# Weighted one-hot matrices built on VectorE alone, and expert products, row gathers and their pace moved between the last three stages

## The chip, the cores and the metric

The kernel runs on one core of a Trainium2 chip. A core has TensorE (PE; its weight loads are listed apart as PEld), VectorE (DVE), ScalarE (ACT), GpSimd (POOL) and SyncE (SP), and 16 DMA engines. Plain transfers are issued from SP's queue, indirect gathers from POOL's. The metric is device microseconds of one execution; the figure for a version is the median of its runs.

## The reference

A two-layer transformer block is followed by a second block, whose last part is the mixture of experts below. Everything that the change touches lies there. 512 tokens (s) have width 1024 (d); there are 8 heads, 128 x 128 = 16384 experts, and 16 experts are picked for each token and head.

```
def peer_ffn(h, w_query, sub_keys, expert_u, expert_v):
    ...
        q = (x_blk @ w_query).reshape(b, t, PEER_HEADS, 2, HALF_KEY)
        scores = jnp.einsum('bthcd,hcnd->bthcn', q, sub_keys).astype(jnp.float32)
        top_s, top_i = lax.top_k(scores, PEER_TOPK)
        cand_s = top_s[..., 0, :, None] + top_s[..., 1, None, :]
        cand_i = top_i[..., 0, :, None] * N_KEYS + top_i[..., 1, None, :]
        ...
        best_s, pos = lax.top_k(cand_s, PEER_TOPK)
        expert_idx = jnp.take_along_axis(cand_i, pos, axis=-1)
        gate = jax.nn.softmax(best_s, axis=-1)
        u = expert_u[expert_idx]
        v = expert_v[expert_idx]
        act = jax.nn.gelu(jnp.einsum('btd,bthkd->bthk', x_blk, u).astype(jnp.float32), approximate=False)
        return jnp.einsum('bthk,bthkd->btd', (gate * act).astype(v.dtype), v)
```

## The kernel before

Everything is float32; a product is made of three matmuls on a high and a low part (`split`: ScalarE rounds the high part, VectorE or GpSimd subtracts it to get the low part). The four blocks of 128 tokens are treated in two ways.

- The first block (object `PA`, `NG = 1`) **gathers**: for each of its 8 x 16 picks an indirect DMA on POOL's queue (`gather`, L1517) brings 128 rows of `peer_u` (one for each token, 128 x 1024 f32, 0.52 MB) into a tile `u`, and VectorE multiplies and sums them with the token rows (`score`, L1531). After 128 of these come `weights`, and 128 gathers of `peer_v` rows that VectorE adds up (`combine`, L1596). The tiles come from a ring of `UD = 4` buffers. The gathers keep their order on POOL (`in_order`).
- The other three blocks (`NV = 3`, 384 tokens) are **dense**. `scores` multiplies all 16384 rows of `peer_u` with the tokens, in 32 groups of 512 experts: a group is two calls of `load_w` with two halves of 128x1024 each (tiles `raw`, `whi`, `wlo`; in this stage GpSimd makes the `wlo` of one half and VectorE that of the other) and 2 x 2 x 8 x 3 = 96 matmuls of 384 columns. The scores go to DRAM (`Sd`). `one_hots` turns the picks into a weight matrix: for four tokens at a time (96 batches) VectorE compares an index row `iota` with the two key indices (`oe`, `oq`, 128 x 4 x 128), ScalarE scales `oe` by the weight, token by token, and TensorE multiplies the two (L1564, 8 matmul records a batch). The result goes to DRAM (`Gd`). `experts` then loads, for each group, the weights (`gt`) and scores (`s`), multiplies them (L1655), splits them (`gh`, `gl`), splits four 128x1024 slices of `peer_v` (`vh`, `vl`) and runs 4 x 3 x 2 x 3 = 72 matmuls of 512 columns (L1682 to L1684) into six PSUM banks that are kept to the end.

The code is written by generators that take turns: `alongside(main, others)` always advances the one with the smallest ratio of steps done to its number, and ends with `main`. Three such stages end the program:

```
        alongside((PB.queries(), 91), (scores_, S_1), (gather_a, G_1))
        alongside((spread(), 69 * NV), (scores_, S_2), (gather_a, G_2))
        for _ in scores_:
            pass
...
        alongside((experts(fp), 32 * 9), (gather_a, max(10, G_3 - G_1 - G_2)))
```

They are called here the **queries** stage (routing of the last two blocks: products with `w_query`, top-16 searches and decoding on VectorE, tiles `ts`, `cand`, `oh`), the **spread** stage (one-hots) and the **experts** stage. `scores` has two steps a group, so `S_1, S_2 = 20, 40` puts 10 groups beside the queries and 20 beside the one-hots; `G_1, G_2, G_3 = 60, 80, 260` do the same for the gathers. A scheduler then sets the final order on each engine; it moves instructions by its own estimate of when they are ready.

Of the kernel before, what the change touches and what calls it, by code (L numbers as in the profile page):

```python
# [14 lines left out]
AF = mybir.ActivationFunctionType  # L15
OP = mybir.AluOpType
AX = mybir.AxisListType
PSUM = bass.MemoryType.PSUM

NO_SYNC = mybir.DependencyInfo(mybir.DependencyClass.NoSync, mybir.DependencyReason.DATA)  # L20

S, D, KT = 512, 1024, 8
# [29 lines left out]
UB = 6  # L52
F_1, F_2, F_3, F_4, L_4 = 1, 36, 2, 20, 1
L_A = 0.01
S_1, S_2, G_1, G_2, G_3 = 20, 40, 60, 80, 260
N_1 = 0
ORD = 1
NU = 32
NG = 1
NV = S // 128 - NG  # L60
# [131 lines left out]
def build(tc, A, out, stop=None, dump=None):  # L192
# [3 lines left out]
    with ctx:  # L196
# [37 lines left out]
        def in_order(i):  # L234
            tc.keep_in_program_order(i)
# [319 lines left out]
        with tc.tile_pool(name="l0", bufs=1) as lp:  # L555
# [97 lines left out]
            for g in range(4):  # L653

                src, n = us[g], 1
# [729 lines left out]
        def normed(q0, w, xh, xl, xs_=None):  # L1385
# [17 lines left out]
            for k in range(KT):  # L1403
# [2 lines left out]
                split(xh[:, k], xl[:, k], h)  # L1406
                yield

        class Peer:
            def __init__(self, h, xh, xl, pool, ng):  # L1410
                self.xh, self.xl, self.ng = xh, xl, ng
                self.q0, self.t0, self.sl = h.q0, h.t0, h.sl
                self.h2 = [hp.tile([128, D], F, name="h2", bufs=ng) for _ in range(ng)]
                self.sd = [pe.tile([128, 8, 16], F, name="sd", bufs=ng) for _ in range(ng)]
                self.ix = [pe.tile([128, 8, 16], I32, name="ix", bufs=ng) for _ in range(ng)]
                self.bs, self.i1, self.i2 = ([pool.tile([128, 8, 16], F, name=n, bufs=2) for _ in range(NT)]
                                             for n in ("bs", "i1", "i2"))
                self.idx, self.ti, self.bp = {}, {}, {}

            def rows(self, t):  # L1420
# [93 lines left out]

            def gather(self, table, t, hd, j):
                u = ring[0]()
                i = GP.indirect_dma_start(out=u, out_offset=None, in_=A[table],  # L1517
                                          in_offset=bass.IndirectOffsetOnAxis(ap=self.idx[t, hd][:, j:j + 1], axis=0))
                if ORD:
                    in_order(i)  # L1520
                return u

            def score(self):
# [26 lines left out]
            def one_hots(self, t):  # L1550
# [17 lines left out]
                for c in range(4):  # L1568
                    st = dp.tile([128, 128, 32], F, name="st", bufs=2)
                    for b in range(8):  # L1570
                        q = dp.tile(full, F, name="oq", bufs=3)
                        e = dp.tile(full, F, name="oe", bufs=3)
                        cut = slice(c * 32 + b * 4, c * 32 + b * 4 + 4)
                        io = iota[:, None, :].to_broadcast(full)
                        V.tensor_tensor(e, io, T[:, 0, cut][:, :, None].to_broadcast(full), op=OP.is_equal)
                        for n in range(4):
                            SC.activation(e[:, n], e[:, n], AF.Copy, scale=T[:, 2, cut][:, n:n + 1])
                        V.tensor_tensor(q, io, T[:, 1, cut][:, :, None].to_broadcast(full), op=OP.is_equal)
                        pend.append((q, e, st[:, :, b * 4:b * 4 + 4]))
                        yield  # L1580
                        if len(pend) > 1:
                            finish()
                        yield
# [44 lines left out]
        def experts(pl):  # L1628
# [43 lines left out]
            def products(g):  # L1672

                gh, gl, vs = st.pop(g)
                for e in range(4):
                    h, l = vs[e]
                    end = g == order[-1] and e == 3
                    for t in range(NV):
                        ts = slice(t * 128, t * 128 + 128)
                        for c in range(2):  # L1680
                            p, cs = acc[t][c], slice(c * 512, c * 512 + 512)
                            PE.matmul(p, gh[:, e, ts], h[:, cs], start=False, stop=False, skip_group_check=True)  # L1682
                            PE.matmul(p, gh[:, e, ts], l[:, cs], start=False, stop=False, skip_group_check=True)  # L1683
                            PE.matmul(p, gl[:, e, ts], h[:, cs], start=False, stop=end, skip_group_check=True)  # L1684
                            if end:
# [83 lines left out]
        dps.close()  # L1769
        fin_ = ExitStack()  # L1770
        fp = fin_.enter_context(tc.tile_pool(name="fp", bufs=1))
        alongside((experts(fp), 32 * 9), (gather_a, max(10, G_3 - G_1 - G_2)))
        for _ in gather_a:
            pass
        fin_.close()
# [28 lines left out]
```

## Time and profile before

| | us |
|---|---|
| median of 3 runs (range) | 3069.81 (3062.46 to 3075.19) |
| the profiled execution | 3066.25 |
| its span, first to last instruction | 3064.5 |
| PE busy in the span | 2896.3 (95%) |
| DVE, ACT, POOL busy in the span | 2155.9 (70%), 1374.7 (45%), 1153.7 (38%) |
| queries stage, first product with `yh` to the end of decoding | 1785 to 2105 |
| spread stage, to the last score product | 2105 to 2508 |
| experts stage, first product to the last | 2514 to 3061 |
| POOL's wait in the experts stage for VectorE to give back a ring buffer | 172.5 |

Matmuls are pipelined and a busy PE need not be PE at its peak: the distance between the starts of equal matmuls tells more than their share of busy time. A duration printed by the trace overlaps the next instruction's by some 0.08 us on DVE, so there too the distance between starts is what an instruction occupies.

### The profile page before, as it was taken

The numbers are of one execution on the slowest core, as the hardware profiler recorded it, in microseconds if no ns is written. First come the engines' busy times: TensorE is split into PE (matmuls) and PEld (weight loads), VectorE is DVE, ScalarE is ACT, GpSimd is POOL, SyncE is SP. The second block draws the span as 40 slices with busy tenths as digits, with TensorE's granted clock in tenths as the row PEclk, the third lists the DMA queues.
The fourth block names the chain that finished last, engine by engine and source line by source line (L and its number), as shares of the span: only waits on it lengthen the run. The fifth ranks groups of instructions, "written<-read, shape, count | busy, mean of one in ns | idle before, by whom it ended". The sixth has DMA issues, their size and how long they took to land.

```text
span 3064.5 us, 44596 instructions
## 1 busy us (share of the span) xinstructions
PE 2896.3 (95%) x16770; PEld 2545.5 (83%) x16770; DVE 2155.9 (70%) x3873; ACT 1374.7 (45%) x2363; POOL 1153.7 (38%) x722
## 2 busy tenths in 40 slices
PE   8999999999989898989789989889999999999999
PEld 6568888878789898789787689889999998777887
DVE  6854344498766737658985668998778758888753
ACT  4533223477454545444354433346666643333332
POOL 3110000344310475467554146555555444454200
PEclk9999999999999999999999889999999999999999
DMA  3122232311245443235342058777787889999964
GB/s 132 41 77 96 87 106 85 101 69 42 62 166 191 162 145 111 83 135 181 120 147 87 18 183 301 248 260 281 294 296 278 302 321 385 371 375 377 333 226 145
DMA packets 195881, 568.29 MB, mean 185 GB/s; under 512 B 16944, under 2 KB 68528, under 8 KB 194000
## 3 DMA queue, kind: packets, MB, share of 16 engines
q1 hardware_dynamic: 157664, 427.61, 40.1%
q0 software_dynamic: 37712, 137.71, 12.1%
q8 instruction: 132, 2.16, 0.3%
q14 instruction: 85, 0.70, 0.1%
q10 hardware_dynamic: 288, 0.11, 0.0%
HBM read 512.93 MB, written 52.43 MB: 184 GB/s over the span
## 4 chain that ended last, share of the span: by engine, by line
PE 72%; DVE 16%; issue 3%; DMA 3%; ACT 3%; POOL 1%; SPq 0%; ACTq 0%; POOLq 0%; DVEq 0%
PE ps L269 15%; PE ps L271 15%; PE ps L270 15%; PE ps L1683 5%; PE ps L1684 5%; PE ps L1682 5%; PE ps L1564 3%; DVE wlo L232 2%; DVE u L1531 2%; POOL wlo L232 1%; PE ps L487 1%; DMA u<-in_peer_u_dram,ix 1%; DMA u<-in_peer_v_dram,ix 1%; PE ps L1173 1%; DVE nm L457 1%
## 5 line engine op out<-in xcount | busy, mean ns | idle before, releaser
L232 POOL TENSOR_TENSOR wlo<-raw,whi 128x1024 fp32r<-128x1024 f32 (+2 forms) x240 | 589.7, 2465 | 597.6 <-ACT whi L231 550.9
L231 ACT ACTIVATE whi<-raw 128x1024 fp32r<-128x1024 f32 (+2 forms) x518 | 515.6, 998 | 634.9 <-PE ps L270 366.2
L232 DVE TENSOR_TENSOR wlo<-raw,whi 128x1024 fp32r<-128x1024 f32 (+3 forms) x278 | 346.9, 1249 | 220.0 <-ACT whi L231 219.6
L271 PE MATMUL ps<-yh,wlo 128*128 128x384 f32 (+1 forms) x1152 | 385.9, 336 | 27.5 <-DVE wlo L232 26.3
L269 PE MATMUL ps<-yh,whi 128*128 128x384 f32 (+1 forms) x1152 | 389.9, 339 | 0.0
L270 PE MATMUL ps<-yl,whi 128*128 128x384 f32 (+1 forms) x1152 | 384.5, 334 | 0.0
L1683 PE MATMUL ps<-vl,gh 128*128 128x512 f32 x768 | 302.6, 394 | 2.0 <-DVE vl L232 1.7
L1684 PE MATMUL ps<-vh,gl 128*128 128x512 f32 x768 | 300.7, 392 | 0.0
L269 PE MATMUL ps<-XH,whi 128*128 128x512 f32 (+1 forms) x680 | 270.7, 403 | 8.6 <-ACT whi L231 8.6
L1517 POOL DMA_INDIRECT u<-in_peer_v_dram,ix x128 | 197.9, 1546 | 203.3 <-DVE h L1596 177.5
L270 PE MATMUL ps<-XL,whi 128*128 128x512 f32 (+1 forms) x680 | 267.9, 397 | 0.0
L271 PE MATMUL ps<-XH,wlo 128*128 128x512 f32 (+1 forms) x680 | 263.0, 395 | 1.8 <-DVE wlo L232 1.8
L1682 PE MATMUL ps<-vh,gh 128*128 128x512 f32 x768 | 242.1, 395 | 9.3 <-ACT vh L231 9.2
L271 PEld LDWEIGHTS ps<-yh,wlo 128*128 128x128 f32 x1152 | 219.9, 191 | 32.4 <-DVE wlo L232 31.0
L231 ACT ACTIVATE vh<-raw 128x1024 fp32r<-128x1024 f32 x128 | 133.1, 1054 | 243.6 <-DMA raw<-in_peer_v_dram 164.6
L1531 DVE SCALAR_TENSOR_TENSOR u<-u,h 128x1024 f32<-128x1024 f32 x127 | 189.0, 1494 | 49.2 <-DMA u<-in_peer_u_dram,ix 49.2
L270 PEld LDWEIGHTS ps<-yl,whi 128*128 128x128 f32 x1152 | 220.5, 191 | 0.0
L269 PEld LDWEIGHTS ps<-yh,whi 128*128 128x128 f32 x1152 | 220.3, 191 | 0.0
L269 PE MATMUL ps<-fx,whi 128*128 128x256 f32 x704 | 200.7, 290 | 6.5 <-ACT fx L353 4.4
L369 POOL TENSOR_TENSOR sqa<-sqa,sq 128x512 f32<-128x512 f32 (+1 forms) x28 | 40.8, 1457 | 439.4 <-ACT sq L367 438.5
L271 PE MATMUL ps<-fx,wlo 128*128 128x256 f32 x704 | 195.0, 286 | 6.5 <-DVE wlo L232 4.3
L270 PE MATMUL ps<-fx,whi 128*128 128x256 f32 x704 | 197.9, 285 | 0.3 <-DVE fx L354 0.3
(428 smaller groups left out, 7120.8 us busy)
## 6 DMA issues: line engine op xcount, KB each, us to landing
raw<-in_uT_dram SPq DMA_DIRECT2D x128, 512.0 KB
raw<-in_peer_v_dram SPq DMA_DIRECT2D x128, 512.0 KB
raw<-in_w_gate_dram SPq DMA_DIRECT2D x66, 512.0 KB
raw<-in_w_up_dram SPq DMA_DIRECT2D x66, 512.0 KB
raw<-in_w_in_dram SPq DMA_DIRECT2D x52, 512.0 KB
Sd<-s SPq DMA_DIRECT2D x32, 768.0 KB
Gd<-st SPq DMA_DIRECT2D x12, 2048.0 KB
gt<-Gd SPq DMA_DIRECT2D x32, 768.0 KB
```

The lines of the kernel that those rows point to most:

```text
L231: SC.activation(hi, src, AF.Copy)
L232: eng.tensor_sub(lo, src, hi.bitcast(F))
L269: PE.matmul(out, wh, xh, start=first, stop=False)
L270: PE.matmul(out, wh, xl, start=False, stop=False)
L271: PE.matmul(out, wl, xh, start=False, stop=last)
L369: GP.tensor_add(self.acc, self.acc, q)
L1517: i = GP.indirect_dma_start(out=u, out_offset=None, in_=A[table], in_offset=bass.IndirectOffsetOnAxis(ap=self.idx[t, hd][:, j:j + 1], axis=0))
L1531: V.scalar_tensor_tensor(u, u, 1.0, self.h2[t], op0=OP.mult, op1=OP.mult, accum_out=self.sd[t][:, hd, j:j + 1])
L1564: PE.matmul(p[:, n * 128:(n + 1) * 128], q[:, n], e[:, n], start=True, stop=True)
L1682: PE.matmul(p, gh[:, e, ts], h[:, cs], start=False, stop=False, skip_group_check=True)
L1683: PE.matmul(p, gh[:, e, ts], l[:, cs], start=False, stop=False, skip_group_check=True)
L1684: PE.matmul(p, gl[:, e, ts], h[:, cs], start=False, stop=end, skip_group_check=True)
```

## The change

Three things are changed. The `oe` matrix is compared and weighted by one VectorE `tensor_scalar` for each token (128x128; two scalars per partition, index and weight) in place of one `tensor_tensor` for four tokens (128x512) and four ScalarE activations. The numbers `S_1, S_2, G_1, G_2` put 17 groups of scores and 45 gathers beside the queries, 15 groups and 60 gathers beside the one-hots, and spread all gathers that are left evenly over the steps of `experts`. And from the second group of expert products on, each gather waits for the first matmul of the group before the one beside which it is written.

```diff
+SYNC = mybir.DependencyInfo(mybir.DependencyClass.Sync, mybir.DependencyReason.SCHED_ONLY)
...
-S_1, S_2, G_1, G_2, G_3 = 20, 40, 60, 80, 260
+S_1, S_2, G_1, G_2 = 34, 30, 45, 60
...
+        PACE = []
...
+                self.taken = 0
...
             def gather(self, table, t, hd, j):
                 u = ring[0]()
+                self.taken += 1
...
                 if ORD:
                     in_order(i)
+                if len(PACE) > 1:
+                    tc.add_manual_dep(i.ins, PACE[-2], SYNC, reason="one group of products ahead")
                 return u
...
-                        V.tensor_tensor(e, io, T[:, 0, cut][:, :, None].to_broadcast(full), op=OP.is_equal)
                         for n in range(4):
-                            SC.activation(e[:, n], e[:, n], AF.Copy, scale=T[:, 2, cut][:, n:n + 1])
+                            V.tensor_scalar(e[:, n], iota, T[:, 0, cut][:, n:n + 1], T[:, 2, cut][:, n:n + 1],
+                                            op0=OP.is_equal, op1=OP.mult)
...
-                            PE.matmul(p, gh[:, e, ts], h[:, cs], start=False, stop=False, skip_group_check=True)
+                            i = PE.matmul(p, gh[:, e, ts], h[:, cs], start=False, stop=False, skip_group_check=True)
+                            if e == t == c == 0:
+                                PACE.append(i.ins.name)
...
-        alongside((experts(fp), 32 * 9), (gather_a, max(10, G_3 - G_1 - G_2)))
+        alongside((experts(fp), 32 * 9 + NV), (gather_a, max(10, 256 * NG - PA.taken)))
```

The orders on the engines are the same up to the queries stage. Lines of the changed kernel stand up to 9 lower than before (L232 is L233, L1531 is L1538).

On VectorE in the queries stage, before: two `wlo` (each belongs to half a `load_w`, so to 48 matmuls) and what stands between them: parts of the routing (`bs`, `i`, `tf`, `bp`, `z`), gathered rows (`u,sd`) and a one-hot batch.

```order
L232 TENSOR_TENSOR wlo<-raw,whi 128x1024
L1470 MAX bs<-cand 128x8
L1531 SCALAR_TENSOR_TENSOR u,sd<-u,h_12662 128x1024
L1575 TENSOR_TENSOR oe<-iota,T_19776 128x512
L1578 TENSOR_TENSOR oq<-iota,T_19776 128x512
L1531 SCALAR_TENSOR_TENSOR u,sd<-u,h_12662 128x1024
L1506 TENSOR_REDUCE i_17161<-oh 128x64
L1492 CAST tf<-ti 128x128
L1471 MAX_INDEX bp<-bs,cand 128x8
L1539 COPY z<-bs 128x8
L232 TENSOR_TENSOR wlo<-raw,whi 128x1024
```

The same place now:

```order
L233 TENSOR_TENSOR wlo<-raw,whi 128x1024
L1506 TENSOR_TENSOR oh<-af,iota 128x1024
L1538 SCALAR_TENSOR_TENSOR u,sd<-u,h_12662 128x1024
L1509 TENSOR_TENSOR oh<-oh,tf 128x1024
L1474 MAX ts<-sc 128x8 x2
L1510 TENSOR_REDUCE i_17161<-oh 128x64
L1475 MAX_INDEX ti<-ts,sc 128x8 x2
L1476 MATCH_REPLACE sc<-ts,sc 128x128 x2
L1477 MAX ts<-sc 128x8 x2
L233 TENSOR_TENSOR wlo<-raw,whi 128x1024
```

There is one gathered row between them in place of two and no one-hot batch; up to the last decoding VectorE's order has 42 `wlo` (33 before), 48 `u,sd` (69), 18 of the small `oe` instructions (12 large ones before) and 4 `oq` (12).

On VectorE in the spread stage, before, from one `wlo` to the next:

```order
L232 TENSOR_TENSOR wlo<-raw,whi 128x1024
L1531 SCALAR_TENSOR_TENSOR u,sd<-u,h_12662 128x1024 x2
L1575 TENSOR_TENSOR oe<-iota,T_22634 128x512
L1578 TENSOR_TENSOR oq<-iota,T_22634 128x512
L1575 TENSOR_TENSOR oe<-iota,T_22634 128x512
L1578 TENSOR_TENSOR oq<-iota,T_22634 128x512
L1548 TENSOR_TENSOR bs<-bs,sd 128x128
L232 TENSOR_TENSOR wlo<-raw,whi 128x1024
```

And now, the same kind of place:

```order
L233 TENSOR_TENSOR wlo<-raw,whi 128x1024
L1538 SCALAR_TENSOR_TENSOR u,sd<-u,h_12662 128x1024
L1583 TENSOR_SCALAR oe<-iota,T_21725 128x128 x4
L1585 TENSOR_TENSOR oq<-iota,T_21725 128x512
L1538 SCALAR_TENSOR_TENSOR u,sd<-u,h_12662 128x1024
L1583 TENSOR_SCALAR oe<-iota,T_21725 128x128 x4
L1585 TENSOR_TENSOR oq<-iota,T_21725 128x512
L1583 TENSOR_SCALAR oe<-iota,T_21725 128x128 x4
L1585 TENSOR_TENSOR oq<-iota,T_21725 128x512
L1538 SCALAR_TENSOR_TENSOR u,sd<-u,h_12662 128x1024
L233 TENSOR_TENSOR wlo<-raw,whi 128x1024
```

Each `oe` row has become four instructions, and more batches stand between two `wlo`. Behind the last decoding and ahead of the first `s<-s,gt` the order holds 366 small `oe`, 92 `oq`, 65 `u,sd`, 29 `wlo` and 3 `vl` (before: 84 `oe`, 84 `oq`, 58 `u,sd`, 12 `h`, 37 `wlo`).

On POOL in the experts stage, before, with the semaphores that each gather waits for (DMASW: the ring of software DMA semaphores; DVE: a tile of the ring is free):

```order
L1517 DMA u<-in_peer_v_dram,ix 128x1024 [waits DMASW6_49,DVE_49]
L1517 DMA u<-in_peer_v_dram,ix 128x1024 [waits DMASW7_49,DVE_49]
L1517 DMA u<-in_peer_v_dram,ix 128x1024 [waits DMASW0_49,DVE_49]
L1517 DMA u<-in_peer_v_dram,ix 128x1024 [waits DMASW1_49,DVE_49]
L1517 DMA u<-in_peer_v_dram,ix 128x1024 [waits DMASW2_49,DVE_49]
```

And now:

```order
L1522 DMA u<-in_peer_v_dram,ix 128x1024 [waits DMASW1_49,DVE_49]
L1522 DMA u<-in_peer_v_dram,ix 128x1024 [waits DMASW2_49,DVE_49]
L1522 DMA u<-in_peer_v_dram,ix 128x1024 [waits DMASW3_49,DVE_49,PE_49]
L1522 DMA u<-in_peer_v_dram,ix 128x1024 [waits DMASW4_49,DVE_49]
L1522 DMA u<-in_peer_v_dram,ix 128x1024 [waits DMASW5_49,DVE_49]
```

One gather in four or five now also waits for TensorE, once a group. Behind the first `s<-s,gt` VectorE's order holds 14 `u,sd` and 128 `h` (before: 116 `h`), and the last of them stands six `vl` ahead of the end.

## Rows read from the trace of the kernel before

**Rows 1.** Windows: stretch, us, then busy us (count) of PE, PEld, DVE, ACT, POOL, PEclk, DMA share, GB/s

```profile
1785.00:2105.00 320.00, 290.78 (x1759) 285.61 (x1760) 290.69 (x671) 128.88 (x222) 181.22 (x104) 0.97 0.74 257
2105.00:2508.00 403.00, 402.96 (x2545) 402.56 (x2545) 301.40 (x340) 252.47 (x584) 198.72 (x110) 1.00 0.81 294
2508.00:2600.00 92.00, 91.47 (x426) 75.78 (x426) 76.96 (x59) 30.95 (x29) 41.43 (x27) 1.00 1.02 384
2600.00:2871.00 271.00, 260.30 (x1102) 210.11 (x1101) 226.30 (x178) 83.78 (x76) 131.67 (x84) 0.97 1.01 374
2871.00:3061.00 190.00, 188.99 (x833) 155.82 (x831) 93.98 (x70) 64.52 (x61) 1.87 (x1) 1.00 0.62 208
```

**Rows 2.** Waits of PE, 1785 to 2105: in total, times, longest

```profile
PE ps L271 <- DVE wlo L232: 26.3, 16, 3.2
```

**Rows 3.** Waits of PE, 2508 to 3062

```profile
PE ps L1682 <- ACT vh L231: 9.2, 4, 2.3
```

**Rows 4.** Timeline of PE, three places: start, duration, instruction

```profile
1838.59 0.28 PE L269 MATMUL ps<-yh,whi 128*128 128x256 f32 x1
...
1839.83 0.28 PE L271 MATMUL ps<-yh,wlo 128*128 128x256 f32 x1
...
2442.85 0.34 PE L270 MATMUL ps<-yl,whi 128*128 128x384 f32 x1
...
2451.06 1.95 PE L1564 MATMUL ps<-oe,oq 128*128 128x128 f32 x16
2452.76 0.42 PE L269 MATMUL ps<-yh,whi 128*128 128x384 f32 x1
...
3029.72 0.39 PE L1684 MATMUL ps<-vh,gl 128*128 128x512 f32 x1
...
3042.41 0.39 PE L1683 MATMUL ps<-vl,gh 128*128 128x512 f32 x1
```

**Rows 5.** Groups by form on DVE, 1785 to 2105

```profile
L1531 DVE SCALAR_TENSOR_TENSOR u<-u,h 128x1024 f32<-128x1024 f32 x69 | 100.2, 1455 | 17.9 <-DMA u<-in_peer_u_dram,ix 17.9
L232 DVE TENSOR_TENSOR wlo<-raw,whi 128x1024 fp32r<-128x1024 f32 x33 | 57.5, 1742 | 5.3 <-ACT whi L231 5.3
```

**Rows 6.** Groups by form on DVE, 2105 to 2508

```profile
L1531 DVE SCALAR_TENSOR_TENSOR u<-u,h 128x1024 f32<-128x1024 f32 x58 | 88.8, 1541 | 31.3 <-DMA u<-in_peer_u_dram,ix 31.3
L1578 DVE TENSOR_TENSOR oq<-iota,T 128x512 f32<-128x512 f32 x85 | 78.0, 917 | 0.0
L1575 DVE TENSOR_TENSOR oe<-iota,T 128x512 f32<-128x512 f32 x85 | 71.6, 843 | 5.7 <-PE ps L1564 5.7
L232 DVE TENSOR_TENSOR wlo<-raw,whi 128x1024 fp32r<-128x1024 f32 x38 | 53.1, 1397 | 51.0 <-ACT whi L231 51.0
```

**Rows 7.** Timeline of DVE in the spread stage

```profile
2240.78 1.23 DVE L1531 SCALAR_TENSOR_TENSOR u<-u,h 128x1024 f32<-128x1024 f32 x1 [1.36 <-DMA u<-in_peer_u_dram,ix]
...
2241.98 1.23 DVE L232 TENSOR_TENSOR wlo<-raw,whi 128x1024 fp32r<-128x1024 f32 x1
2243.12 0.69 DVE L1575 TENSOR_TENSOR oe<-iota,T 128x512 f32<-128x512 f32 x1
2243.72 2.90 DVE L1578 TENSOR_TENSOR oq<-iota,T 128x512 f32<-128x512 f32 x1
2246.54 0.68 DVE L1575 TENSOR_TENSOR oe<-iota,T 128x512 f32<-128x512 f32 x1
```

**Rows 8.** Timeline of POOL at the same time

```profile
2243.35 2.71 POOL L232 TENSOR_TENSOR wlo<-raw,whi 128x1024 fp32r<-128x1024 f32 x1 [5.51 <-ACT whi L231]
```

**Rows 9.** Timeline of DVE, two earlier places with `tensor_scalar` by scalars per partition

```profile
1121.74 0.72 DVE L1147 TENSOR_SCALAR pj<-pj,lb,lb 128x256 f32<-128x256 f32 x2
1122.39 0.28 DVE L1159 TENSOR_SCALAR hg_k<-pj 128x256 f32<-128x256 f32 x1
1122.59 0.27 DVE L1188 TENSOR_TENSOR hg_qs<-pj 128x128 f32<-128x128 f32 x1
...
1740.10 0.35 DVE L1300 TENSOR_SCALAR me<-me,rs 128x256 f32<-128x256 f32 x1
1740.36 0.75 DVE L232 TENSOR_TENSOR xl<-mix,xh 128x256 fp32r<-128x256 f32 x2
```

## The prediction

> **What bounds the kernel now.** The program is the same up to 1785 us, so I read the rest, first by windows. In the queries stage (1785 to 2105) VectorE is busy 290.7 of 320 us, TensorE has gaps of 29 us and its granted clock is 0.97; in the spread stage TensorE is busy without a gap at clock 1.00 and VectorE 301 of 403; in the experts stage TensorE has its gaps while the DMA engines are full (share 1.01 to 1.02, 374 to 384 GB/s) and hardly any afterwards, when the share is 0.62 [rows 1]. The reader is to see that TensorE always has most to do, and that a different partner holds it up in each stage. The waits name the partners: the low parts `wlo` from VectorE in the queries stage (26.3 us in 16 waits), the high parts `vh` in the experts stage (9.2 us), and those come after `raw` loads [rows 2, 3].
>
> Busy time hides how much of it is work, so I take the work from the distance of equal matmuls: 47 of them in 8.21 us, 0.1747 us for 384 columns; 0.1127 for 256 columns (11 in 1.24); 0.106 for one record of a one-hot product (16 in 1.70); 0.2266 for 512 columns (56 in 12.69) [rows 4]. Queries and spread together hold 32 groups x 96 = 3072 score matmuls (536.7 us), 8 x 2 x 8 x 3 = 384 query matmuls (43.3) and 768 + 64 one-hot and key records (88.2): 668 us in a stretch of 723. So 55 us are lost, nearly all in the queries stage, since the spread stage has neither gap nor slow clock. The experts stage is 2304 x 0.2266 = 522 us and 48 transposes, 527 of 553: 26 us lost. All that the change can win is some 80 us, if it costs nothing.
>
> **The queries stage.** 17 groups instead of 10 come with it, so TensorE's work there is 17 x 96 x 0.1747 = 285, 43 for the queries and 10 for keys and the first one-hots: 339 us. VectorE's share changes by the counts of the order: 21 gathered rows fewer at 1.455 us, 9 `wlo` more at 1.742 [rows 5], 12 large `oe` and 8 `oq` fewer at 0.843 and 0.917 [rows 6], 18 small `oe` more: 290.7 - 30.6 + 15.7 - 10.1 - 7.3 + 4.7 = 263 us. It was 91% of its stage and becomes 78% of TensorE's 339. The two stages of the trace give the bounds for what TensorE still loses: about nothing at VectorE 75% (the spread stage), some 48 us at 91%. 78% is near the first, but routing comes in bursts of several us ahead of a `wlo`, so I take 15 us, and 5 and 48 as ends: 354 us (344 to 387).
>
> **The spread stage.** TensorE's work becomes 15 x 96 x 0.1747 = 251 and 92 x 8 x 0.106 = 78, with a few transposes 331 us. VectorE loses a cheap instruction and gets four dear ones. From start to start, a gathered row takes 1.20 us, a `wlo` 1.14 and an `oe` or `oq` 0.60 [rows 7]. A two-scalar `tensor_scalar` on 128x128 stands nowhere in the trace. On 128x256 two of them take 0.65, so 0.325 each, one with one scalar 0.26 and one with constants 0.20 [rows 9]: each scalar adds about 0.06. The width's share is unknown. If nothing shrinks, the price is 0.325; if a column costs as much as between `oe` and `wlo` (0.54 us for 512 columns, so 0.135 for 128), it is 0.19. As 0.20 for 256 columns is already less than that slope gives for the columns alone (0.27), I take half the shrinkage, 0.26. A batch's `oe` then rises from 0.60 to 1.04 us.
>
> To this comes the contention with GpSimd: an `oq` that starts 0.4 us into a GpSimd `wlo` of 2.71 us takes 2.90 instead of 0.68 [rows 7, 8]. Over the stage the excess of the means over the free durations is 58 x 0.31 + 85 x 0.24 + 85 x 0.16 + 38 x 0.17 = 58 us for 38 pairs of halves [rows 6], 1.5 us a pair; with 29 pairs left, 44 to 64 us (all at 2.2), I take 50. So VectorE needs 65 x 1.20 + 92 x 0.60 + 32 x 1.14 = 170, with contention 220, with 366 x 0.26 = 95 for `oe` 315 us, and it waited 31 us for gathered rows [rows 6]; a busier engine meets more of them landed, so 20: 335 us against TensorE's 331. Two engines equally long and tied by few buffers lose something to each other: I take 346. The ends are 337 (0.19: VectorE 305, as little lost as now) and 370 (0.325 and the whole 31 us).
>
> The Trainium skill, page "SBUF — State Buffer", section "SBUF: two separate sides", says that VectorE and GpSimd share a pair of ports under an exclusive lock, taken for a whole instruction by a VectorE operation with two SBUF inputs or in a two-port mode, the loser waiting. The 2.90 us row agrees for two inputs. By that rule the one-input `tensor_scalar` is blocked too and the 50 us stay, as summed; did it not lock, only the other 170 of 265 us could be hit, VectorE would need 18 us less, and TensorE's 331 would bound. The rule also has them hold up GpSimd's descriptor writing. Nothing of the sum rests on this paragraph.
>
> ScalarE loses 384 activations and is busy 252 of 403 us at present [rows 1], so that is off the path; it makes `whi` earlier, and VectorE's 51 us of waiting for it [rows 6] can shrink, which is why I count none of it.
>
> Both stages: 354 + 346 = 700 instead of 723, **-23 us** (681 to 757).
>
> **The experts stage.** 142 gathers of 0.52 MB are combined in it instead of 116. It moved 384 x 92 + 374 x 271 + 208 x 190 = 176 MB [rows 1]; with 26 x 0.524 it is 190 MB. Before, its gathers ran as fast as ring and VectorE let them and were over at 2871: while they ran, DMA was full and TensorE did 1102 x 0.2266 = 250 us of work in 271 [rows 1], 21 lost. Now they are spread over the stage: 190 MB in some 540 us is 352 GB/s, 94% of the full rate of 374. That is the gain and the risk: no stretch asks for more than there is, but there is no calm one either. Ends: 3 us lost (as after 2871), or 527 x 21/271 = 41 if it runs like the full stretch all along; I take 14, nearer to the first since demand stays under the rate. So **-12 us** (-23 to +15). VectorE's work rises by 26 rows of 1.2 us in a stage where it was busy 397 of 553 us, which covers it; without that cover it would be 31 us late.
>
> The new wait on TensorE costs nothing by itself. Behind a waiting gather stand only further gathers, and their readers on VectorE, behind which stand `vl`. But it waits for the group before the one it is written beside, which started a whole group (72 x 0.2266 = 16 us) earlier, and the ring usually holds it longer. If a row came late nonetheless, VectorE would stop at it and the next `vl` would be late. At the end, six `vl` follow the last row, so nothing hangs over.
>
> **Sum.** 3066.25 for the profiled execution - 23 - 12 = 3031; the median of the runs is 3.6 us above that execution, so 3035 for a median.
>
> **Rivals.** *Slower: VectorE bounds the spread stage.* Nothing of the small `oe` shrinks with the width and successive ones do not overlap: 0.72 for two less the start distance of 0.325 is 0.395 for one [rows 9]. Then 220 + 145 + 31 = 396 us, 354 + 396 - 723 - 12 = +15, with the queue losses between two engines some 18: 3088. It decides from 0.39 us an instruction. For it: 366 new instructions, VectorE already level with TensorE. Against: on DVE successive instructions overlap in every row [rows 7].
>
> *No change: what the queries stage wins, the spread stage gives back.* At 0.325, VectorE needs 370 and a little for the queue: 354 + 375 - 723 - 12 = -6, 3064. *No change: DMA bounds the whole experts stage*, +15 instead of -12: 3062. For it: 94% of the full rate with no pause. Against: after 2871 nothing was lost at 0.62.
>
> *Everything is won.* TensorE waits for nobody: 681 in place of 723, and 23: -65, 3005. For it: the spread stage shows that such a state exists; against: VectorE would have to stay below TensorE in bursts too.
>
> **Numbers.** The forecast (3014 to 3054) has 0.50, everything won 0.14, given back 0.19, DMA-bound 0.05, slower 0.12. About 0.5% (15 us) is what a measurement of this kernel can tell from no change. So faster 0.64, same 0.24, slower 0.12; median 3035. To leave out no more than 0.2, the range goes from 3003, just under everything won, to 3084, just under the slower rival. The forecast's own range is 3014 to 3054.
>
> **What would show it.** Right: the stretch to the end of decoding grows to about 354 us and TensorE's waits for `wlo` fall below half of 26.3; the one-hots end some 23 us earlier than now; the small `oe` starts every 0.26 us; the DMA share in the experts stage is near 0.95 to its end with no stretch of lost TensorE work over 5%. Wrong: small `oe` at 0.33 or more, and TensorE waiting for `wlo`, `oe` or `oq` in the spread stage; waits for `vh` above 20 us in the experts stage; gathers that land after the last product.

## The result, and the profile after

The changed kernel is slower: median 3107.07 us (3095.04 to 3113.8, six runs) against 3069.61 before (six runs), ratio 1.013 (95% interval 1.011 to 1.0151). The forecast was 3035 in a range of 3003 to 3084. The profiled execution took 3113.44 us, with a span of 3111.7.

First the windows, cut by stage where rows 1 were: the queries stage to the end of decoding, the spread stage to the first transposes, then the experts stage in three. Columns as in [rows 1].

```profile
1785.00:2158.00 373.00, 355.98 (x2138) 352.03 (x2139) 268.01 (x643) 139.88 (x209) 175.33 (x92) 0.98 0.66 227
2158.00:2531.00 373.00, 343.23 (x2162) 341.29 (x2161) 317.78 (x613) 134.97 (x210) 145.28 (x91) 0.97 0.72 262
2531.00:2600.00 69.00, 57.85 (x272) 48.51 (x271) 50.94 (x58) 21.92 (x20) 18.83 (x14) 0.90 0.98 351
2600.00:2871.00 271.00, 263.02 (x1141) 215.56 (x1140) 216.09 (x168) 86.48 (x80) 111.59 (x75) 0.99 0.97 356
2871.00:3107.00 236.00, 222.34 (x953) 180.67 (x951) 170.92 (x133) 72.33 (x68) 81.21 (x53) 0.98 0.86 312
```

The spread stage, without a gap and at a granted clock of 1.00 before [rows 1], now has 30 us of gaps at 0.97. The experts stage, to the last product at 3107, takes 577 us; cut by the same events (first transposes to last product) it took 552 before, and the two stages ahead 724 (319 and 405) against 746 now. Together that is the 47 us by which the two profiled executions differ.

TensorE's waits in the three stages (the answers to [rows 2, 3]; the second had none before):

```profile
PE ps L272 <- DVE wlo L233: 9.1, 9, 2.9
PE ps L1571 <- DVE oq L1585: 5.9, 1, 5.9
PE ps L324 <- DVE rcol L304: 5.1, 1, 5.1
...
PE ps L1571 <- DVE oq L1585: 29.8, 12, 3.5
...
PE ps L1689 <- ACT vh L232: 20.9, 7, 3.9
PE ps L1689 <- ACT gh L232: 11.2, 1, 11.2
```

The wait for `wlo` fell as forecast. New are those for `oq`, most of it in the spread stage, and for `gh` ahead of the first expert product; that for `vh` behind it has grown from 9.2 [rows 3] to 20.9. VectorE's groups by form, the first row from the queries stage, the others from the spread stage (the answers to [rows 5, 6]):

```profile
L1538 DVE SCALAR_TENSOR_TENSOR u<-u,h 128x1024 f32<-128x1024 f32 x48 | 76.5, 1599 | 71.3 <-DMA u<-in_peer_u_dram,ix 71.3
...
L1583 DVE TENSOR_SCALAR oe<-iota,T 128x128 f32<-128x128 f32 x368 | 158.0, 491 | 34.6 <-PE ps L1571 31.0 <-ACT T L1563 3.4
L1538 DVE SCALAR_TENSOR_TENSOR u<-u,h 128x1024 f32<-128x1024 f32 x61 | 80.4, 1324 | 10.6 <-DMA u<-in_peer_u_dram,ix 10.3
L1585 DVE TENSOR_TENSOR oq<-iota,T 128x512 f32<-128x512 f32 x92 | 62.5, 679 | 0.0
L233 DVE TENSOR_TENSOR wlo<-raw,whi 128x1024 fp32r<-128x1024 f32 x29 | 35.3, 1218 | 6.2 <-ACT whi L232 6.2
```

In one stage TensorE waits for VectorE's `oq` (29.8 us) while VectorE waits for TensorE to give `oe` back (31.0): neither is the bound, the buffers between them are. One place shows it, on VectorE, TensorE and GpSimd in turn (timelines; the answer to [rows 7, 8]):

```profile
2295.74 1.11 DVE L1583 TENSOR_SCALAR oe<-iota,T 128x128 f32<-128x128 f32 x4
2296.77 0.68 DVE L1585 TENSOR_TENSOR oq<-iota,T 128x512 f32<-128x512 f32 x1
...
2309.44 1.21 DVE L233 TENSOR_TENSOR wlo<-raw,whi 128x1024 fp32r<-128x1024 f32 x1
2313.01 3.27 DVE L1583 TENSOR_SCALAR oe<-iota,T 128x128 f32<-128x128 f32 x4 [2.36 <-PE ps L1571]
2316.21 0.68 DVE L1585 TENSOR_TENSOR oq<-iota,T 128x512 f32<-128x512 f32 x1
...
2311.92 2.84 PE L1571 MATMUL ps<-oe,oq 128*128 128x128 f32 x24
2317.03 1.13 PE L1571 MATMUL ps<-oe,oq 128*128 128x128 f32 x8 [2.27 <-DVE oq L1585]
...
2313.08 2.35 POOL L233 TENSOR_TENSOR wlo<-raw,whi 128x1024 fp32r<-128x1024 f32 x1 [5.98 <-ACT whi L232]
```

All three buffers are full until TensorE begins its three batches (24 records) at 2311.92; VectorE, idle since about 2310.6, starts the fourth batch when the first comes free, meets GpSimd's `wlo`, and TensorE waits 2.27 us for it. The small `oe` themselves cost what was forecast: four from 2295.74 to 2296.77, 0.257 us each.

The start of the experts stage (TensorE, SP's queue, VectorE, ScalarE):

```profile
2536.50 1.04 PE L1612 MATMUL ps<-ident,X 128*128 128x128 f32 x8
2548.69 0.79 PE L1689 MATMUL ps<-vh,gh 128*128 128x512 f32 x1 [11.15 <-ACT gh L232]
...
2523.65 0.33 SPq L1593 DMA_DIRECT2D Gd<-st  x1
...
2532.80 0.38 SPq L1653 DMA_DIRECT2D gt<-Gd  x1
2533.22 4.76 SPq L1656 DMA_DIRECT2D s<-Sd  x1
...
2545.00 1.76 DVE L1662 TENSOR_TENSOR s<-s,gt 128x1536 f32<-128x1536 f32 x1 [3.25 <-DMA s<-Sd]
...
2547.17 1.47 ACT L232 ACTIVATE gh<-s 128x1536 fp32r<-128x1536 f32 x1
```

The last weights are stored at 2523.65, reloaded from 2532.80, multiplied at 2545.00 and rounded at 2547.17, while TensorE has nothing but the transposes. The store takes some 9 us to land. Of the two loads behind it the one for the scores, issued second on the same queue, lands last: VectorE's wait of 3.25 us ends with it. Before, the last one-hot product came at 2475 and two groups of scores stood behind it, to 2508, so that this way was covered.

### The profile page after: what moved, and what is told of

It is laid out like the page before. It is cut to its first block, busy times and chain, and to the rows that moved or that the text cites. A ratio compares the mean times of both kernels' runs of the same rounds, so it can differ in the third digit from the quotient of the medians.

```text
span 3111.7 us, 44368 instructions
## 1 busy us (share of the span) xinstructions
PE 2905.4 (93%) x16770; PEld 2552.9 (82%) x16770; DVE 2188.9 (70%) x4161; ACT 1270.5 (41%) x1979; POOL 1130.8 (36%) x722
## 4 chain that ended last, share of the span: by engine, by line
PE 60%; DVE 18%; DMA 10%; issue 8%; ACT 2%; POOL 1%; SPq 0%; DVEq 0%; POOLq 0%; ACTq 0%
PE ps L270 15%; PE ps L272 15%; PE ps L271 15%; DMA u<-in_peer_v_dram,ix 6%; DMA u<-in_peer_u_dram,ix 3%; PE ps L1571 2%; DVE wlo L233 2%; PE ps L488 1%; PE ps L1692 1%; PE ps L1693 1%; PE ps L1689 1%; DMA raw<-in_peer_v_dram 1%; DVE h L1603 1%; DVE u L1538 1%; PE ps L1174 1%
## 5 line engine op out<-in xcount | busy, mean ns | idle before, releaser
L232 ACT ACTIVATE whi<-raw 128x1024 fp32r<-128x1024 f32 (+2 forms) x518 | 516.6, 999 | 826.5 <-PE ps L271 569.9
L233 POOL TENSOR_TENSOR wlo<-raw,whi 128x1024 fp32r<-128x1024 f32 (+2 forms) x240 | 578.9, 2420 | 710.0 <-ACT whi L232 687.4
L233 DVE TENSOR_TENSOR wlo<-raw,whi 128x1024 fp32r<-128x1024 f32 (+3 forms) x278 | 335.8, 1210 | 196.8 <-ACT whi L232 196.4
L1689 PE MATMUL ps<-vh,gh 128*128 128x512 f32 x768 | 244.3, 397 | 32.0 <-ACT vh L232 20.9
L1538 DVE SCALAR_TENSOR_TENSOR u<-u,h 128x1024 f32<-128x1024 f32 x127 | 178.6, 1413 | 97.0 <-DMA u<-in_peer_u_dram,ix 96.7
L232 ACT ACTIVATE vh<-raw 128x1024 fp32r<-128x1024 f32 x128 | 132.0, 1054 | 214.4 <-DMA raw<-in_peer_v_dram 156.8
L1603 DVE SCALAR_TENSOR_TENSOR h<-u,bs,h 128x1024 f32<-128x1024 f32 x128 | 164.4, 1284 | 77.4 <-DMA u<-in_peer_v_dram,ix 76.6
L270 PE MATMUL ps<-fx,whi 128*128 128x256 f32 x704 | 199.9, 289 | 6.1 <-ACT fx L354 4.2
```

Source lines behind the costliest of these rows:

```text
L232: SC.activation(hi, src, AF.Copy)
L233: eng.tensor_sub(lo, src, hi.bitcast(F))
L270: PE.matmul(out, wh, xh, start=first, stop=False)
L1538: V.scalar_tensor_tensor(u, u, 1.0, self.h2[t], op0=OP.mult, op1=OP.mult, accum_out=self.sd[t][:, hd, j:j + 1])
L1603: V.scalar_tensor_tensor(ac, v, self.bs[t][:, hd, j:j + 1], ac, op0=OP.mult, op1=OP.add)
L1689: i = PE.matmul(p, gh[:, e, ts], h[:, cs], start=False, stop=False, skip_group_check=True)
```

## The experiments

Theories at the start: A, the 366 small `oe` overload VectorE; B, the pace makes rows late. When both had fallen as the main cause, the four numbers were taken apart (C, where the groups of scores stand; D, where the gathers stand), and then the ring of three `oe`/`oq` buffers. Stage times are those of one profiled execution, which can stand 11 us from the median. Ratios are against the kernel before, run beside each experiment (medians of 3066 to 3068 us).

### Each part alone, and each left out

**One-hots alone**: before, with the four `tensor_scalar` in place of `tensor_tensor` and activations.

> The kernel before with the small tensor_scalar one-hots alone; numbers and gathers as before. Theory A (the one-hots cost time because GpSimd's wlo blocks them just when TensorE waits for the batch): TensorE gets waits for oq in the spread stage, some 15 to 30 us, and the time is 3080 to 3095. Rival (the one-hots are harmless while TensorE has 20 groups beside them; the moved numbers do the harm): no such waits, 3060 to 3073.

3070.18, ratio 1.0001 (0.998 to 1.0022). Queries and spread take 739 us in a profiled execution 10 us above the median, with no waits in the spread stage. A falls: alone they cost nothing measurable.

**The change without its one-hots**:

> The changed kernel with the one-hots of before (one compare of 512 columns and four ScalarE activations); numbers and pacing as changed. Theory A: the spread stage loses its 30 us of waits for oq, 3075 to 3085. Rival (numbers): the one-hots still come late, the stage keeps most of its loss, 3098 to 3110.

3106.96, 1.0136 (1.0082 to 1.019): as slow as the change, with 32.3 us of waits for `oq`.

**The change without the pace**:

```diff
-                if len(PACE) > 1:
-                    tc.add_manual_dep(i.ins, PACE[-2], SYNC, reason="one group of products ahead")
```

> The changed kernel without the gathers' wait for TensorE. Theory B (the wait makes the peer_v rows late: VectorE waited 77 us for them in the experts stage and the vl behind them are late): those waits fall below 25 us, the experts stage shrinks by 15 to 30 us, 3077 to 3092. Rival (the experts stage is slow because 26 more gathers share the DMA engines with the loads): the stage stays within 6 us, 3101 to 3112.

3100.63, 1.0115 (1.0083 to 1.0147). The experts stage falls from 577 to 565 us and the waits for `vh` from 20.9 to 7.2, though that for `gh` grows from 11.2 to 17.9. Most of the loss stays: B is a part at most. The 6 us between the medians are not clear of noise, for the interval of the change (1.011 to 1.0151) overlaps this one.

**The numbers alone**: before, with `S_1, S_2, G_1, G_2 = 34, 30, 45, 60` and the even spread of the rest.

> The kernel before with the new numbers alone (17 and 15 groups, 45 and 60 gathers, the rest spread evenly over the expert products), one-hots as before, no wait for TensorE. If theories A and B explain the loss, it is about as fast as before or faster, 3045 to 3075. Rival (the numbers do the harm, by a late end of the one-hots and by rows that come late in the queries stage): 3080 to 3105.

3105.44, 1.0115 (1.0071 to 1.0159), with waits for `oq` of 34.1 and for `gh` of 18.7 us. The numbers by themselves make the loss, or nearly all of it.

**Of the numbers, the groups alone** (`S_1, S_2 = 34, 30`, all else of before), **and the gathers alone** (45 and 60, the rest evenly, 20 and 40 kept):

> The kernel before with 17 and 15 groups of scores beside the queries and the one-hots (10 and 20 before), its own 60, 80 and 260 for the gathers, no pace, its own one-hots. The four numbers alone (both groups and gathers) gave 3105. Theory 'groups' (the loss lies in where the score groups stand: too few beside the one-hots and none behind them): 3095 to 3110, with the wait of TensorE for oq in the spread stage at 25 to 35 us and for gh before the first expert product at 10 to 18. Theory 'gathers' (later rows: more of them in the experts stage): 3070 within 6, with those two waits small.

> The kernel before with 45 and 60 gathers beside the queries and the one-hots and all others spread evenly over the products, its own 10 and 20 groups of scores, no pace, its own one-hots. Theory 'groups': 3070 within 8, the spread stage without waits of TensorE, the experts stage about as before (552). Theory 'gathers': 3090 to 3105, with the experts stage at 565 to 578.

Groups: 3085.16, 1.006 (1.0041 to 1.008), waits for one-hots 29 us in the spread stage and 17.8 for `gh`. Its loss lies in the first two stages (745 us for 724); the experts stage takes 550 us in spite of the wait for `gh`, since the waits for `vh` there are 0.8 in place of 9.2. Gathers: 3073.13, 1.0011 (0.9986 to 1.0036), neither wait, but an experts stage of 560 us. C is the larger part, though at 3085 it missed its expected 3095 or more. Groups and gathers together cost some 13 us more than the two apart (1.0115 against 1.006 and 1.0011); the interval of 1.0115 is so wide that this excess may be nothing, and no run shows a cause for it.

**The pace alone** (old numbers and one-hots):

> The kernel before with the pace of the gathers alone (its numbers and one-hots). The paced version lost 6 us against the unpaced one with the new numbers. If the pace by itself makes rows late: 3075 to 3082, with VectorE's waits for rows of peer_v in the experts stage at 60 to 80 us (under 20 without pace). If it only costs where more gathers stand beside the products: 3070 within 4.

3073.92, 1.0023 (1.0005 to 1.0041). VectorE waits 75.5 us for `peer_v` rows instead of 7.0, yet TensorE's experts stage is as long as before (552), so the profiled execution does not show where the time went.

**Two groups of scores left behind the one-hots**: the numbers alone with `S_2 = 26`.

> The four numbers with 13 groups of scores beside the one-hots in place of 15, so that two groups (33 us of products) are left behind the last one-hot batch, as before the change; no pace, the one-hots of before. Theory 'groups, by the end' (the last weights' way through DRAM lies open before the first product): the wait for gh falls from 18.7 us to under 3 and the time from 3105 to 3085 to 3092. Theory 'groups, by the one-hots' (too few scores beside 96 batches): the wait for gh falls too, but the waits for oq grow (more batches a group), so 3098 to 3110. Theory 'gathers': 3105 within 6.

3118.58, 1.0159 (1.0131 to 1.0187). The wait for `gh` is gone and the experts stage is 16 us shorter (553 for 569), but the waits for one-hots are 51 us. Batches a half group (48 score matmuls) and waits go together: before, the 371 us from 2104 to 2475 hold 2362 matmuls, 679 of them one-hots, so 85 batches beside 35 halves, 2.4 each, and no wait; 92 beside 30 are 3.1, and 30 us; 92 beside 26 are 3.5, and 51 us. There are three buffers.

### The ring

**The change with five buffers**:

```diff
-                        q = dp.tile(full, F, name="oq", bufs=3)
-                        e = dp.tile(full, F, name="oe", bufs=3)
+                        q = dp.tile(full, F, name="oq", bufs=5)
+                        e = dp.tile(full, F, name="oe", bufs=5)
```

> The changed kernel with five buffers each for oe and oq in place of three. Theory 'ring' (some batches of a half group find no one-hot matrix made ahead, because three buffers hold three batches and a half group of scores now has 3.2 beside it): TensorE's waits for oq in the spread stage fall from 29.8 us to under 8 and VectorE's waits for TensorE to give oe back from 31 to under 8; the 12 us without products before the first expert product stay, so 3080 to 3092. Rival 'VectorE' (it has no time left beside rows and wlo, whatever the buffers): the waits for oq stay over 20 us, or as much comes back as waits for wlo, and the time is 3102 to 3112.

3086.29, 1.0074 (1.0049 to 1.01). Its windows, spread and experts stage, VectorE's `oe` in the spread stage, and TensorE's waits in the experts stage:

```profile
2146.00:2480.00 334.00, 333.51 (x2170) 332.62 (x2169) 304.55 (x611) 134.01 (x212) 164.37 (x90) 1.00 0.79 291
2480.00:3076.00 596.00, 550.16 (x2359) 447.02 (x2358) 438.81 (x359) 180.78 (x169) 216.27 (x143) 0.96 0.90 327
```

```profile
L1583 DVE TENSOR_SCALAR oe<-iota,T 128x128 f32<-128x128 f32 x366 | 125.9, 411 | 0.8 <-PE ps L1571 0.8
```

```profile
PE ps L1689 <- ACT vh L232: 27.8, 9, 4.8
PE ps L1689 <- ACT gh L232: 12.3, 1, 12.3
PE ps L1692 <- DVE vl L233: 5.0, 10, 1.6
```

The spread stage falls from 373 to 334 us, without a gap and at a clock of 1.00, against 331 of work as forecast. The rival (no time left on VectorE) falls. Queries and spread take 695 us, where 700 had been forecast; in two later runs with the same groups, gathers and five buffers they take 703 and 711. What remains is the experts stage, at 596.

**Groups of the change on the kernel before, with five buffers; the same with two groups left behind; and the kernel before with five buffers alone**:

> The kernel before with 17 and 15 groups of scores (3085 with three buffers) and five buffers each for oe and oq. Theory 'ring': the waits for one-hots in the spread stage fall from 29 us to under 8, the wait for gh (17.8) stays: 3060 to 3070. Rival 'VectorE': 3080 to 3088, with the waits for one-hots over 20 us or as much for wlo.

> The kernel before with 17 and 13 groups of scores, two left behind the one-hots, and five buffers each. With three buffers and the gathers of the change, leaving two made the spread stage worse (waits for one-hots 51 us) and closed the gap before the first product. Theory 'ring': both losses go, and the stages give 724 us at most from the first product of the queries to the first transposes and 550 after: 3055 to 3068. Rival 'VectorE': waits for one-hots of 25 us or more, 3080 to 3095.

> The control: the kernel before (10 and 20 groups) with five buffers each for oe and oq. It has no wait for one-hots in its spread stage, so by theory 'ring' nothing can be gained: 3067 within 5. If the buffers help by something else (fewer waits for wlo in the queries stage), under 3058.

3057.14, 0.9965 (0.9943 to 0.9987); 3056.53, 0.9957 (0.994 to 0.9974); 3075.37, 1.0028 (1.0011 to 1.0045). The control gains nothing; it is a little slower than the kernel before and came out some 3 us over what was expected of it. The ring costs only where the groups are moved: 28 us with the groups of the change (3085 to 3057), nothing with those of before. Leaving two groups took the wait for `gh` away and made the experts stage 10 us shorter (542 for 552), but cost as much ahead (the first transposes 13 us later).

### What is left in the experts stage

**Five buffers without pace; that with two groups left; and the same two groups with the pace**:

> The changed kernel with five buffers each for oe and oq and without the pace. With five buffers and pace the first two stages took 695 us to the first transposes and the experts stage 596, against 565 without pace and 577 with it on three buffers. Theory 'pace' (gathers held until the products reach a group, then VectorE waits for their rows and hands vl and vh on late): the experts stage falls to 560 to 568 and the time from 3086 to 3052 to 3062, under the kernel before. Rival 'rows' (142 gathers at DMA share near 1 cost the same whenever they are issued): the experts stage stays at 580 or more, 3075 to 3086.

> As the run before (five buffers, no pace), with 13 groups of scores beside the one-hots in place of 15, so that two are left behind the last one-hot. Theory 'gap' (the way of the last weights through DRAM lies open, 12 to 18 us): the wait for gh falls under 3 us and the time is 3040 to 3050. If the spread stage gives back in waits for one-hots what the gap gains, as it did with the gathers of before (3056 against 3057): 3052 to 3062.

> The changed kernel, pace and all, with five buffers and two groups of scores left behind the one-hots. Theory 'pace': 20 to 30 us above the same without pace, with VectorE's waits for rows of peer_v at 70 us or more. Rival 'rows': within 6 us of it.

3055.3, 0.9962 (0.9944 to 0.9981); 3062.45, 0.9984 (0.9968 to 1.0); 3070.18, 1.0009 (0.999 to 1.0027). The first beats both kernels, though by no more than the groups and the ring alone (3057). With two groups left the wait for `gh` is gone again, but not to 3040 to 3050: the spread stage takes 350 us in place of 334, with 9.3 us of waits for `oq`, and the experts stage 562 in place of 559. The first one's windows (two stretches of the experts stage, then the whole of it) and TensorE's waits there:

```profile
2560.00:2700.00 140.00, 140.00 (x619) 115.91 (x619) 119.72 (x93) 47.32 (x42) 75.87 (x44) 1.00 1.03 381
2700.00:2850.00 150.00, 148.34 (x647) 120.57 (x646) 131.57 (x103) 49.59 (x45) 81.20 (x48) 1.00 1.04 389
...
2496.00:3055.00 559.00, 535.78 (x2362) 439.38 (x2360) 437.58 (x359) 184.16 (x169) 240.99 (x143) 0.98 0.95 349
```

```profile
PE ps L1687 <- ACT gh L232: 15.2, 1, 15.2
PE ps L1687 <- ACT vh L232: 4.0, 4, 2.3
PE ps L1690 <- DVE vl L233: 2.9, 5, 1.5
```

Without the pace the same 143 gathers run at a DMA share of 1.03 and 1.04 in these two stretches, with hardly a gap on TensorE and a clock of 1.00. So it was not the number of rows. With two groups left the pace cost 8 us, not the 20 to 30 expected; the two intervals overlap, VectorE's waits for rows are 54 us, not 70, and the profiled experts stages are alike (561 with the pace, 562 without), so these 8 us are not clear of noise.

The prediction took it that the ring usually holds a gather longer than the pace. In the experts stage of the changed kernel POOL waits for both, but mostly for TensorE; before, its waits for the ring were 172.5 us:

```profile
POOL u L1522 <- PE ps L1689: 218.2, 26, 20.5
POOL u L1522 <- DVE h L1603: 63.9, 27, 5.6
```

How the pace can stop TensorE shows in the changed kernel (timelines of POOL, VectorE, ScalarE and TensorE):

```profile
2812.09 0.95 POOL L1522 DMA_INDIRECT u<-in_peer_v_dram,ix  x1 [0.58 <-DVE h L1603]
2824.60 1.98 POOL L1522 DMA_INDIRECT u<-in_peer_v_dram,ix  x1 [11.56 <-PE ps L1689]
...
2814.54 1.28 DVE L1603 SCALAR_TENSOR_TENSOR h<-u,bs,h 128x1024 f32<-128x1024 f32 x1 [2.72 <-DMA u<-in_peer_v_dram,ix]
2818.31 1.28 DVE L1603 SCALAR_TENSOR_TENSOR h<-u,bs,h 128x1024 f32<-128x1024 f32 x1 [2.49 <-DMA u<-in_peer_v_dram,ix]
2819.51 1.75 DVE L1662 TENSOR_TENSOR s<-s,gt 128x1536 f32<-128x1536 f32 x1
...
2821.35 1.48 ACT L232 ACTIVATE gh<-s 128x1536 fp32r<-128x1536 f32 x1 [13.13 <-DVE s L1662]
2822.74 2.93 ACT L232 ACTIVATE vh<-raw 128x1024 fp32r<-128x1024 f32 x3
...
2823.83 2.35 PE L1689 MATMUL ps<-vh,gh 128*128 128x512 f32 x6 [3.44 <-ACT vh L232]
```

Two rows land late, and VectorE waits 2.72 and 2.49 us for them; behind these two `h` stands `s<-s,gt` on VectorE, behind that `gh` on ScalarE, behind that `vh`, and TensorE waits 3.44 us for it. The next gathers wait for that TensorE (11.56 us), so one lateness can bring on the next.

**The pace with one group more room** (`PACE[-3]`), **and the one-hots of the change on the groups of the change, gathers of before, five buffers, no pace**:

> The changed kernel with five buffers and the pace, but each gather waits for the first matmul of the group two before the one beside which it is written (one before in the change). Paced by one it took 3086, without pace 3055. Theory 'late rows' (the wait lets a row start so late that VectorE stops for it, and s, gh and vh stand behind): one group, 16 us, more room makes the rows land in time, VectorE's waits for rows of peer_v fall from 85 us to under 40 and the time is 3055 to 3065. Rival 'burst' (the pace gathers four or five issues behind one matmul, whenever it comes): waits and time stay, 3080 to 3090.

> The kernel before with the one-hots of the change, 17 and 15 groups of scores and five buffers each, its own gathers, no pace. With the one-hots of before this took 3057, with the gathers of the change and its one-hots 3055. If one-hots on VectorE and later gathers are both neutral once the ring is mended: 3050 to 3060. If the later gathers gain something that the dearer one-hots on VectorE cost: 3062 to 3070.

3084.69, 1.0063 (1.0042 to 1.0083): no better than one group ahead, with 82.9 us of waits for rows. POOL still waits 208 us for TensorE (223 with one group), so one group more of room did not free the gathers. The rival, bursts of issues, fits but no run takes a burst apart. 3061.65, 0.9982 (0.996 to 1.0004): against 3057 with the one-hots of before and 3055 with the later gathers too. The one-hots on VectorE can cost some 5 us here and the later gathers give as much back, but the three intervals overlap.

What the later gathers do to the experts stage shows best in runs that have neither pace nor a wait for `gh`. The first three lines have the gathers of the change (the gathers alone; the numbers with two groups left; five buffers, no pace, two groups left), the last those of before (17 and 13 groups, five buffers):

```profile
2512.00:3072.00 560.00, 538.83 (x2361) 439.71 (x2359) 433.61 (x361) 177.71 (x166) 232.74 (x147) 0.99 0.94 345
2562.00:3115.00 553.00, 539.55 (x2361) 440.67 (x2359) 429.98 (x359) 176.65 (x165) 222.70 (x147) 0.99 0.95 347
2506.00:3068.00 562.00, 543.48 (x2358) 443.13 (x2356) 430.10 (x359) 177.08 (x165) 231.05 (x147) 0.98 0.93 340
...
2506.00:3048.00 542.00, 533.98 (x2353) 438.66 (x2352) 389.79 (x300) 177.12 (x163) 171.46 (x110) 0.99 0.88 318
```

The kernel before took 552. The later gathers made this stage no shorter, and the 541 us of the forecast were reached only with the gathers of before.

## Why the prediction was wrong, step by step

The sum was 3031 for the profiled execution, which took 3113. The 82 us between them are 19 in the queries stage, 27 in the spread stage and 36 in the experts stage. In each stage of the changed kernel what is lost is TensorE's waits and, as an estimate, what the lower granted clock takes: (1 - clock) x stage, since a mean of 0.97 between the two levels of 1.2 and 2.4 GHz loses 3% of the stage's work. Work is counted from the stage's matmuls at the prediction's prices. The clock is printed to 0.01, and the sums come within 6 us of the stages.

| stage | work + lost, forecast | measured: work, waits, clock | sum, and stage |
|---|---|---|---|
| queries | 339 + 15 = 354 | 343, 20, 7 | 370 of 373 |
| spread | 331 + 15 = 346 | 326, 30, 11 | 367 of 373 |
| experts, from the first transposes | 527 + 14 = 541 | 527, 33, 17 | 577 of 577 |

- **Right: the price of the small `oe`** (0.26 taken, 0.257 measured) **and VectorE's load** in the spread stage: 335 us with 20 of waiting for rows; with five buffers it is 305 busy and 27 waiting, and the stage takes 334. The rival that priced `oe` at 0.39 is refuted, though the result came out on its side.
- **Right: GpSimd's contention stays.** The four `oe` at 2313.01 take 3.20 us to the next start, under a GpSimd `wlo`, in place of 1.03. The Trainium skill, page "SBUF — State Buffer", section "SBUF: two separate sides", lets a GpSimd operation that reads SBUF and a VectorE one with two SBUF inputs or in a two-port mode exclude each other for a whole instruction; the trace agrees, here for an operation with one tensor input.
- **Wrong: "Two engines equally long and tied by few buffers lose something to each other: I take 346."** The mechanism was right, the term mis-sized: 41 us lost in waits and clock, not 15. I compared the engines' totals over the stage; what decides is how many batches stand beside one half group (3.1) against three buffers. Five buffers took all of it back.
- **Wrong: "Both stages: 354 + 346 = 700 instead of 723."** This let the experts stage begin where the spread stage ends. Putting all 32 groups beside other work took away the two that stood behind the last one-hot and hid the weights' way through DRAM: 11 us without a matmul in the change, and a lower clock behind it. What the gap costs in the end is not shown: closing it by leaving two groups made the experts stage 16 and 10 us shorter in two pairs of runs and 3 us longer in a third, and the stages ahead took as much or more, so no total fell beyond the noise. With the ring mended the 700 nearly held (695, 703 and 711), and the gap stayed (waits for `gh` of 12 to 15 us).
- **Wrong: "The new wait on TensorE costs nothing by itself."** With five buffers it cost 31 us; the 6 in the change and the 8 each with old numbers and with two groups left are near the noise. The reason given, that "the ring usually holds it longer", was false: POOL waited 218 us for TensorE and 64 for the ring. I had also not followed the chain behind a late row past `vl`, to `s`, `gh` and `vh`. Why 31 there and 8 or less elsewhere stays open; the two cases with a gap before the first product lost 12 and 37 us of experts stage to the pace, those without none.
- **Wrong: the experts stage's "I take 14", so "-12 us".** The stage lost 50 us (577 against 527): by the table 33 of waits, of which `vh` 21 and the gap 11, and 17 of clock. That is not the pace and the gap alone. In the three runs with the later gathers and neither of them 26 to 35 us were lost (553 to 562), inside the ends of 3 and 41, but no less than before (552). "Now they are spread over the stage" needs the pace: with five buffers and no pace the last `h` starts at 2961, 94 us ahead of the end, and the DMA share is 1.02 to 1.04 from 2500 until then. In the change, with the pace, the last `h` starts at 3083 and the share is 0.95 from 2600 until then, but TensorE stops for `vh` by the chain above. So spreading the rows did not give TensorE back what a full DMA had cost it; what the 26 to 35 us consist of, beyond 12 to 14 of waits for `vh`, was not taken apart.
- **Mis-sized: the queries stage**, 30 lost for 15, inside its range of 344 to 387. Waits for `wlo` fell to 9.1, but VectorE waits 71.3 us for rows (17.9 before [rows 5]) and TensorE 5.9 for a first `oq`. Runs with nearly the same order took 361 to 377; no experiment took this stage apart, so the cause stays open.

Even with ring and pace mended, what is won is 0.4%, not 1.1%. In that profiled execution queries and spread take 711 us for 724 before, where 700 were forecast, and the experts stage 559 for 552, where 541 were.

## What to carry to other kernels

Between two engines of about equal load, count what the producer must have ready for the consumer's longest run, not the totals: with three buffers, 2.4 batches beside a half group cost no waits here, 3.1 some 30 us and 3.5 some 51. Work that looks free to move may be the cover of a latency at a stage's end; before moving the last of it, write down what has to happen between the two stages and how long that takes. Here the gap came, though closing it gained nothing in any of three tries. A pacing wait on one queue can be paid by whatever stands behind its readers on the in-order engines, so follow that chain until it comes back to the engine waited for, and read from the waits which of two holds binds.

## What was not expected of the hardware

- A wait can be paid one and a half times: with five buffers and pace TensorE's 45 us of waits go with a granted clock of 0.96 over 596 us, some 24 us more. The first expert product after the 11.15 us wait takes 0.79 us, the usual one 0.39 [rows 4]. It is not always so: with the pace alone 15 us of waits in the experts stage, none over 1.7, went with a clock of 1.00.
- A full DMA need not slow TensorE: 140 us at a share of 1.03 with no gap and a clock of 1.00. Yet at shares of 0.93 to 0.95 over the whole stage, in other runs, 26 to 35 us were lost.
